# Seven instead of eight half-matrix products in six chunks of a decoder layer's last product

## The chip, the cores and the metric

The kernel runs on one core of one Trainium2 chip. The metric is the device time of one execution in microseconds (us), the median of several runs. Matrix products run on TensorE (PE in the profile, its weight loads PEld), elementwise work on VectorE (DVE) and ScalarE (ACT), and SyncE (SP) issues most transfers from HBM into SBUF. Results of TensorE go to PSUM, which has eight banks of 128 x 512 numbers.

## What is computed

One decoder layer for 256 tokens of width 1024, everything in float32: a norm, one input projection, two kinds of sparse attention, a gated merge with an output projection, and a feed-forward block with a squared ReLU:

```python
x = x + mixed @ w_out[layer]
h2 = rmsnorm(x, norm2_g[layer])
u = jax.nn.relu(h2 @ w_ff1[layer])       # 1024 -> 4096
x = x + (u * u) @ w_ff2[layer]           # 4096 -> 1024
return rmsnorm(x, norm_f_g)
```

The change concerns the product with w_ff2, called the second product here; the one with w_ff1 is the first.

## The kernel before

**Splitting.** TensorE multiplies in a fast format (float32r) that keeps fewer digits. So each operand is split into a high part (ScalarE copies it into the fast format, line 106) and a low part (VectorE takes the difference, line 108), and a product of two matrices is three matmuls, high x high, high x low, low x high (`mm3`, line 219). All of them are issued at line 217.

**Chunks and slots.** The weights come as 60 chunks of 128 x 2048 numbers (1 MB) in the order of the list CHUNKS. Raw chunks, high parts and low parts have three rotating buffers each. A slot is the stretch in which TensorE works on one chunk (`run_slot`, line 202): a list of matmuls, and a list of events, each a function with a position between 0 and 1. An event is issued among the matmuls at its position. That fixes only the order within each engine's queue; an engine starts its next instruction as soon as what it waits for is there. In slot c `split_events` (line 249) puts the splitting of chunk c + 2, in two halves, and then the load of chunk c + 5 into the raw buffer that this frees. In slots 0 to 14 of the second product `std_events` (line 258) calls it with the usual positions.

**The second product.** Its 16 chunks each hold 256 rows of w_ff2, as two row tiles k of 128 x 1024. The left operand, (relu)^2 transposed, lies in the tiles sqh and sql (high, low), written during the first product by `ff1_evac` (line 829), which runs on ScalarE and VectorE in the slot behind its own: ReLU, square in place, high part, low part. A chunk adds, to each of four PSUM banks (two halves t of the tokens times two halves of the columns), the product of two 128 x 128 pieces (k = 0, 1) with 128 x 512 pieces of the weights: eight half-matrix products, 24 matmuls (`ff2_mms`, line 873). In the text B11, B12, B21, B22 are the four 128 x 512 quarters of a chunk and A11 to A22 the four 128 x 128 pieces of the left operand.

**Around it.** In slot 1 `x1_rows` (line 789) transposes the residual x into four PSUM banks (acc0, acc1, tp, yb) and ScalarE copies it to SBUF (line 799). In slot 3 `rstd2` (line 842) squares and sums it on ScalarE; VectorE makes the factors of the norm. Slot 14 covers chunks 14 and 15 together, output part by output part, so that `final_a` (line 886) can add each part to the residual, square it and multiply it with the gain while TensorE is at the next part. `first_part` (line 914) does a quarter of it early. `final_b` (line 902) scales rows and sends them out; GpSimd makes the power in between (line 904). The last part's accumulator is the bank yb.

**Placing.** Some tiles are allocated with unused columns between them ("gap"), so that those behind lie at chosen offsets. The tiles h2h and h2l (left operand of the first product) and sqh and sql come from one pool behind such gaps.

Of the kernel before, what the change touches and what calls it, by code (L numbers as in the profile page):

```python
# [8 lines left out]
F32 = mybir.dt.float32  # L9
F32R = mybir.dt.float32r  # L10
AF = mybir.ActivationFunctionType
ALU = mybir.AluOpType
# [15 lines left out]
    + [("ff2", i, 2048) for i in range(16)]  # L28
)
NCH = len(CHUNKS)  # L30
C_Q, C_QM, C_KM, C_VM, C_GM, C_UPN, C_UPM, C_WOUT, C_FF1, C_FF2 = (
    4, 6, 8, 10, 12, 20, 22, 24, 28, 44)

# [6 lines left out]
def hybrid_layer(ctx: ExitStack, tc: tile.TileContext, gxd, w, w1c, small, const, gf, out):  # L40
    nc = tc.nc
    act, dve, pool, pe = nc.scalar, nc.vector, nc.gpsimd, nc.tensor
# [3 lines left out]
    cp = ctx.enter_context(tc.tile_pool(name="cp", bufs=1))  # L46
# [10 lines left out]
    def bank(tag, name):  # L57
        return ps.tile([128, 512], F32, name=name, tag=tag)
# [8 lines left out]
    def acc_tile():  # L67
        return next_bank("acc")
# [12 lines left out]

    raw, hi, lo = {}, {}, {}

    def raw_tile(c):
        raw[c] = wp.tile([128, 2048], F32, name="raw")

# [5 lines left out]
    def load(c):  # L92
        if c < NCH:
            raw_tile(c)
            load_part(c, 0, 1)

    def split(c, part, parts=2, which=""):
        if c >= NCH:
            return
        n = CHUNKS[c][2]  # L100
        if part == 0 and c not in hi:
            hi[c] = wp.tile([128, 2048], F32R, name="whi")
            lo[c] = wp.tile([128, 2048], F32R, name="wlo")
        a, b = part * n // parts, (part + 1) * n // parts
        if which != "l":
            act.activation(hi[c][:, a:b], raw[c][:, a:b], AF.Copy)  # L106
        if which != "h":
            dve.tensor_tensor(lo[c][:, a:b], raw[c][:, a:b], hi[c][:, a:b].bitcast(F32),  # L108
                              op=ALU.subtract)
# [89 lines left out]
    def at(pos, f, *a):  # L199
        ev.append((pos, f, a))  # L200

    def run_slot(mms):
        n = len(mms)
        es = sorted(ev, key=lambda e: e[0])
        ev.clear()
        j = 0
        for i, m in enumerate(mms):
            while j < len(es) and es[j][0] <= i / n:
                es[j][1](*es[j][2])
                j += 1  # L210
            m()
        while j < len(es):
            es[j][1](*es[j][2])
            j += 1

    def mm(o, l, r, start, stop):
        pe.matmul(o, l, r, start=start, stop=stop, skip_group_check=True)  # L217

    def mm3(o, lh, ll, rh, rl, first, last):
        return [lambda: mm(o, lh, rh, first, False),  # L220
                lambda: mm(o, lh, rl, False, False),
                lambda: mm(o, ll, rh, False, last)]
# [16 lines left out]
    def wstat(o, c, off, nk, ncol, ah, al, ks=None, first=0, last=None):  # L239

        r = []
        last = nk - 1 if last is None else last
        for k in (range(nk) if ks is None else ks):
            a = k * ncol + off
            r += mm3(o, hi[c][:, a:a + 128], lo[c][:, a:a + 128], ah[:, k, :], al[:, k, :],
                     k == first, k == last)
        return r

    def split_events(c, hs, ls):
        for i in range(2):  # L250
            at(hs[i], split, c + 2, i, 2, "h")
        for i in range(2):
            if ls[i] <= 1:
                at(ls[i], split, c + 2, i, 2, "l")
        if ls[1] <= 1:
            at(max(ls) + 0.05, load, c + 5)

    def std_events(c):
        if 9 <= c < 20 and c % 2:
            split_events(c, (0.0, 0.06), (0.09, 0.46))  # L260
        elif 9 <= c < 20:
            split_events(c, (0.0, 0.45), (0.3, 0.8))
        else:
            split_events(c, (0.0, 0.45), (0.3, 0.46))
# [335 lines left out]
    for sec, c0, n in groups:  # L600
# [6 lines left out]
        for i in range(2):  # L607
            c = c0 + i
# [56 lines left out]
    for g in range(4):  # L665
        accs = [acc_tile(), acc_tile()]
        for i in range(2):
            c = C_GM + 2 * g + i
# [40 lines left out]
    for sec, c0, kind, evac in (("upn", C_UPN, "n", upn_evac), ("upm", C_UPM, "m", upm_evac)):  # L709
        for i in range(2):  # L710
            c = c0 + i
# [26 lines left out]
    def two_blocks(c, ah, al, late=8):  # L738

        if late < 8:  # L740
            outs = [acc_tile()[:, 0:256] for _ in range(2)]
            whole = None
            order = [range(late), range(late, 8)]
        else:
            whole = acc_tile()
            outs = [whole[:, 0:256], whole[:, 256:512]]
            order = [range(8)]
        mms = []
        for ks in order:
            for m in range(2):  # L750
                mms += wstat(outs[m], c, m * 128, 8, 256, ah, al, ks=ks, last=7)
        return mms, outs, whole
# [3 lines left out]
    FB = {}  # L756

    def open_ff():
        at_stack.close()
        FB["p"] = ctx.enter_context(tc.tile_pool(name="ff", bufs=1))  # L760
        FB["o"] = ctx.enter_context(tc.tile_pool(name="ps_o", bufs=1, space=PS))
        p = FB["p"]
        p.tile([128, 96], F32, name="gap")
        FB["h2h"] = p.tile([128, 8, 256], F32R, name="h2h")
        FB["h2l"] = p.tile([128, 8, 256], F32R, name="h2l")
        p.tile([128, 16], F32, name="gap2")
        FB["sqh"] = p.tile([128, 32, 256], F32R, name="sqh")
        FB["sql"] = p.tile([128, 32, 256], F32R, name="sql")
        FB["gfb"] = p.tile([128, 1024], F32, name="gfb")
        FB["x1"] = p.tile([128, 2, 1024], F32, name="x1")  # L770
        FB["scr"] = p.tile([128, 1024], F32, name="fscr")
        FB["fst"] = p.tile([128, 24], F32, name="fst")
# [28 lines left out]
    for i in range(4):  # L801
        c = C_WOUT + i
# [20 lines left out]
        else:  # L823
            mms, outs, _ = two_blocks(c, mxh, mxl, 4 if i == 0 else 8)
            run_slot(mms)
            prev = [(wout_evac, (i, outs))]


    def ff1_evac(i, outs, whole):
        r = FB["p"].tile([128, 2, 256], F32, name="ur", bufs=2)  # L830
        rf = r.rearrange("p a q -> p (a q)")
        h, l = (FB[n][:, 2 * i:2 * i + 2, :].rearrange("p a q -> p (a q)") for n in ("sqh", "sql"))
        if whole is None:
            for m in range(2):
                act.activation(r[:, m], outs[m], AF.Relu)
        else:
            act.activation(rf, whole, AF.Relu)  # L837
        dve.tensor_tensor(rf, rf, rf, op=ALU.mult)  # L838
        act.activation(h, rf, AF.Copy)  # L839
        dve.tensor_tensor(l, rf, h.bitcast(F32), op=ALU.subtract)  # L840

    def rstd2():
        fst = FB["fst"]
# [5 lines left out]
    for i in range(16):  # L849
        c = C_FF1 + i  # L850
        if i == 0:
            lo_late(0.03, c - 1)
            split_events(c, (0.1, 0.45), (0.5, 0.5))
        else:
            std_events(c)
        for f, a in prev:
            at(0.02, f, *a)
        mms, outs, whole = two_blocks(c, FB["h2h"], FB["h2l"], 6 if i == 0 else 8)
        run_slot(mms)
        prev = [(ff1_evac, (i, outs, whole))]  # L860
# [3 lines left out]
    PARTS = {0: [(0, 0, 512), (0, 512, 512)], 1: [(1, 0, 512), (1, 512, 512)]}  # L864
    LAST = [(1, 512, 256), (1, 768, 256)]
    ops = {p: FB["o"].tile([128, 512], F32, name=f"o{p[0]}_{p[1]}") for p in PARTS[0] + PARTS[1]}
    whole = ops[PARTS[1][1]]
    ops[LAST[0]] = whole
    fst, x1, scr = FB["fst"], FB["x1"], FB["scr"]
    xo = x1  # L870
    xg = gx[:, 16:].rearrange("p (t d) -> p t d", t=2)

    def ff2_mms(i, p):
        c = C_FF2 + i
        t, c0, n = p
        r = []
        for k in range(2):
            kt = 2 * i + k
            lh, ll = (FB[a][:, kt, t * 128:(t + 1) * 128] for a in ("sqh", "sql"))
            a = k * 1024 + c0  # L880
            r += mm3(ops[p][:, 0:n], lh, ll, hi[c][:, a:a + n], lo[c][:, a:a + n],
                     kt == (28 if p == LAST[1] else 0),
                     kt == (27 if p == PARTS[1][1] else 31))
        return r

    def final_a(p, j):

# [30 lines left out]

    order = PARTS[0] + PARTS[1]
    for i in range(15):  # L920
        std_events(C_FF2 + i)
        for f, a in prev:
            at(0.02, f, *a)
        prev = []
        if i == 1:
            at(0.5, x1_rows, range(4), [acc_tile() for _ in range(3)] + [bank("yb", "yb")])
        if i == 3:
            at(0.1, rstd2)
        if i < 14:
            run_slot([m for p in order for m in ff2_mms(i, p)])  # L930
        else:
            ops[LAST[1]] = bank("yb", "yb")
            at(0.05, first_part)
            at(0.23, final_a, PARTS[0][0], 0)
            at(0.43, final_a, PARTS[0][1], 1)
            at(0.46, final_b, 0)
            at(0.64, final_a, PARTS[1][0], 0)
            at(0.83, final_a, LAST[0], 1)
            run_slot([m for p in PARTS[0] + PARTS[1][:1] + LAST for m in ff2_mms(14, p) + ff2_mms(15, p)])
# [88 lines left out]
```

## Time and profile before

| | us |
|---|---|
| runs: median (lowest to highest of 3) | 380.61 (380.51 to 381.44) |
| the profiled execution | 381.45 |
| its span, first to last instruction | 379.7 |
| TensorE busy in it | 369.5 |
| VectorE busy | 254.5 |
| ScalarE busy | 205.5 |

The profile lists one execution. A row of the timeline has the start (us from the span's start), the duration (us), the engine, the source line, the operation, the tile written and the tiles read, the shape and the number of instructions that the row merges; in brackets stands how long the engine was idle before it and what ended the wait. Ends of matmuls are modelled; starts are measured. The profiled execution is 0.84 us longer than the median run.

The first product takes 197 to 284 us, the second 284 to 373 us.

### The profile page before, as it was taken

To read this page: it belongs to the slowest core of one execution; us is meant where nothing else is said; L and a number is where in the kernel's file an instruction comes from. 1 tells how busy PE (TensorE), PEld (TensorE's weight loads), DVE (VectorE), ACT (ScalarE), POOL (GpSimd) and SP (SyncE) were. 2 spreads that over 40 slices of the span, in tenths; PEclk is the share of its full clock that TensorE was granted. 3 is DMA by queue.
4 is the path that set the end of the run, shared out by engine and by line. 5 is a ranking of instruction groups with operands and counts; after the bars stand their busy time and mean duration, and the time that the engine had idled before them with its cause. 6 is when DMAs were issued, how large, how long until landed. Compare 5 with 4: busy or idle time off the path is not lost.

```text
span 379.7 us, 5935 instructions
## 1 busy us (share of the span) xinstructions
PE 369.5 (97%) x2406; PEld 323.6 (85%) x2406; DVE 254.5 (67%) x397; ACT 205.5 (54%) x360; POOL 5.4 (1%) x15
## 2 busy tenths in 40 slices
PE   6999999999999999999999999999999999999993
PEld 5997878878888788779999999999998888888883
DVE  2978878896966869667868657766676254334435
ACT  5975465767746657343555555565556454433412
POOL 2020000000000000000000000000000000000000
PEclk9999999999999999999999999999999999999998
DMA  7996435333533335440755645554456545654003
GB/s 243 365 370 245 155 127 206 110 112 121 203 121 113 110 125 208 166 167 0 272 230 221 224 163 178 216 218 165 181 215 211 194 161 209 221 173 160 1 2 111
DMA packets 10972, 66.38 MB, mean 175 GB/s; under 512 B 1216, under 2 KB 2752, under 8 KB 3648
## 3 DMA queue, kind: packets, MB, share of 16 engines
q1 hardware_dynamic: 10512, 65.21, 47.2%
q10 hardware_dynamic: 432, 0.79, 0.6%
q8 instruction: 19, 0.31, 0.3%
q14 instruction: 9, 0.07, 0.1%
HBM read 64.94 MB, written 1.05 MB: 174 GB/s over the span
## 4 chain that ended last, share of the span: by engine, by line
PE 88%; DVE 4%; ACT 2%; issue 2%; DMA 1%; POOL 1%; SPq 1%; POOLq 0%; DVEq 0%; ACTq 0%
PE acc L217 53%; PE o L217 22%; PE qacc L217 3%; PE yb L217 2%; PE kvbacc L217 2%; DMA raw<-in_kva_dram 1%; DVE wlo L108 1%; ACT whi L106 1%; PE Sb L508 1%; PE Sa L508 1%; PE Sa L217 1%; PE tp L217 1%; PE Sb L217 1%; PE tp L298 1%; POOL rstd L193 0%
## 5 line engine op out<-in xcount | busy, mean ns | idle before, releaser
L106 ACT ACTIVATE whi<-raw 128x1024 fp32r<-128x1024 f32 (+2 forms) x128 | 123.4, 990 | 98.0 <-PE o L217 35.4
L108 DVE TENSOR_TENSOR wlo<-raw,whi 128x1024 fp32r<-128x1024 f32 (+2 forms) x128 | 141.6, 1138 | 43.3 <-ACT whi L106 43.3
L217 PE MATMUL acc<-h2h,whi 128*128 128x256 f32 x256 | 70.7, 276 | 0.0
L217 PE MATMUL acc<-h2l,whi 128*128 128x256 f32 x256 | 70.7, 276 | 0.0
L217 PE MATMUL acc<-h2h,wlo 128*128 128x256 f32 x256 | 70.7, 276 | 0.0
L217 PE MATMUL acc<-whi,hTh 128*128 128x512 f32 (+1 forms) x128 | 50.9, 398 | 1.7 <-ACT whi L106 1.5
L217 PE MATMUL acc<-wlo,hTh 128*128 128x512 f32 (+1 forms) x128 | 50.5, 395 | 0.4 <-DVE wlo L108 0.2
L217 PE MATMUL acc<-whi,hTl 128*128 128x512 f32 (+1 forms) x128 | 49.5, 387 | 0.0
L217 PE MATMUL o<-whi,sqh 128*128 128x512 f32 (+1 forms) x128 | 49.5, 386 | 0.0
L217 PE MATMUL o<-whi,sql 128*128 128x512 f32 (+1 forms) x128 | 49.4, 386 | 0.0
L217 PE MATMUL o<-wlo,sqh 128*128 128x512 f32 (+1 forms) x128 | 49.4, 386 | 0.0
L217 PEld LDWEIGHTS acc<-h2h,wlo 128*128 128x128 f32 x256 | 48.1, 188 | 0.0
L217 PEld LDWEIGHTS acc<-h2l,whi 128*128 128x128 f32 x256 | 48.1, 188 | 0.0
L217 PEld LDWEIGHTS acc<-h2h,whi 128*128 128x128 f32 x256 | 48.1, 188 | 0.0
L217 PEld LDWEIGHTS acc<-whi,hTh 128*128 128x128 f32 x128 | 24.1, 188 | 8.5 <-ACT whi L106 2.2
L217 PEld LDWEIGHTS acc<-wlo,hTh 128*128 128x128 f32 x128 | 24.1, 188 | 5.0 <-DVE wlo L108 1.1
L217 PEld LDWEIGHTS o<-wlo,sqh 128*128 128x128 f32 x128 | 24.0, 188 | 4.9
L217 PEld LDWEIGHTS o<-whi,sqh 128*128 128x128 f32 x128 | 24.0, 188 | 4.8
L217 PEld LDWEIGHTS o<-whi,sql 128*128 128x128 f32 x128 | 24.0, 188 | 4.8
L217 PEld LDWEIGHTS acc<-whi,hTl 128*128 128x128 f32 x128 | 24.1, 188 | 4.3
L838 DVE TENSOR_TENSOR ur<-ur 128x512 f32<-128x512 f32 x16 | 11.1, 693 | 17.2 <-ACT ur L837 16.2
L840 DVE TENSOR_TENSOR sql<-ur,sqh 128x512 fp32r<-128x512 f32 x16 | 11.1, 693 | 11.2 <-ACT sqh L839 11.2
(249 smaller groups left out, 513.3 us busy)
## 6 DMA issues: line engine op xcount, KB each, us to landing
raw<-in_ff_dram SPq DMA_DIRECT2D x32, 1024.0 KB, 4.8
raw<-in_gm_dram SPq DMA_DIRECT2D x8, 1024.0 KB, 4.8
raw<-in_wout_dram SPq DMA_DIRECT2D x4, 1024.0 KB, 4.7
raw<-in_q_dram SPq DMA_DIRECT2D x2, 1024.0 KB, 6.9
raw<-in_qm_dram SPq DMA_DIRECT2D x2, 1024.0 KB, 8.3
raw<-in_km_dram SPq DMA_DIRECT2D x2, 1024.0 KB, 5.5
raw<-in_vm_dram SPq DMA_DIRECT2D x2, 1024.0 KB, 4.7
raw<-in_upn_dram SPq DMA_DIRECT2D x2, 1024.0 KB, 4.8
```

The lines of the kernel that those rows point to most:

```text
L106: act.activation(hi[c][:, a:b], raw[c][:, a:b], AF.Copy)
L108: dve.tensor_tensor(lo[c][:, a:b], raw[c][:, a:b], hi[c][:, a:b].bitcast(F32), op=ALU.subtract)
L217: pe.matmul(o, l, r, start=start, stop=stop, skip_group_check=True)
L298: pe.transpose(tp[:, j * 256 + t * 128:j * 256 + t * 128 + 128], src[:, t, (2 * i + j) * 128:(2 * i + j + 1) * 128], ident)
L508: pe.transpose(S[x][:, j, c:c + 128], P[:, 2 * x + j, c:c + 128], ident)
L838: dve.tensor_tensor(rf, rf, rf, op=ALU.mult)
L840: dve.tensor_tensor(l, rf, h.bitcast(F32), op=ALU.subtract)
```

## The change

In chunks 2, 4, 6, 8, 10 and 12 of the second product, the 2 x 2 block product is formed with seven products in the form of Winograd and Strassen. The left sums (S1 = A21 + A22, S2 = S1 - A11, S3 = A11 - A21, S4 = A12 - S2) are made in the first product, in the event behind `ff1_evac`, and split into high and low parts; S1 takes the place of A21 in sqh and sql, the others go to the space that the first layers' left operands had. The right sums (T1 = B12 - B11, T3 = B22 - B12, T2 = B22 - T1, and T2 less B21 with its sign turned) are made by VectorE in place in the raw chunk, after B11, B21 and B22 have been split; then they are split into two tiles, th and tl, that take the place of h2h and h2l. Three of the seven products are added to the output banks C11, C12, C21 as before; four (P1, P5, P6, P7) are accumulated over all six chunks in the banks yb, acc0, tp and acc1. In slot 13 `seven_sum` combines these four and adds them to the residual, scaled by the norm's factor. The raw buffer of a seven chunk is loaded anew after its T sums have been split, in the slot before its own. Tiles in the pool are placed anew.

```diff
+SEVEN = (2, 4, 6, 8, 10, 12)
...
+        if seven(c):
+            a, b = ((0, 512), (1024, 2048))[part]
...
-        if ls[1] <= 1:
+        if ls[1] <= 1 and not seven(c + 2):
             at(max(ls) + 0.05, load, c + 5)
...
-        p.tile([128, 96], F32, name="gap")
-        FB["h2h"] = p.tile([128, 8, 256], F32R, name="h2h")
-        FB["h2l"] = p.tile([128, 8, 256], F32R, name="h2l")
-        p.tile([128, 16], F32, name="gap2")
+        p.tile([128, 48], F32, name="gap")
+        for n in "hl":
+            FB["h2" + n] = (p.tile([128, 2176 if n == "h" else 2096], F32R, name="h2" + n, tag="h2" + n)[:, 48:2096]
+                            .rearrange("p (k q) -> p k q", k=8))
+        p.tile([128, 80], F32, name="gap2")
...
+    def s_sums(i, r):
...
+        S = [FB["scr"][:, 128 * a:128 * a + 128] for a in range(4)]
+        A = [[r[:, k, 128 * t:128 * t + 128] for k in range(2)] for t in range(2)]
+        for o, x, y, op in ((0, A[1][0], A[1][1], ALU.add), (2, A[0][0], A[1][0], ALU.subtract),
+                            (1, S[0], A[0][0], ALU.subtract), (3, A[0][1], S[1], ALU.subtract)):
+            dve.tensor_tensor(S[o], x, y, op=op)
+
+    def s_split(i):
+        for h, l, v in ((s_tiles(i, "h")[0], s_tiles(i, "l")[0], FB["scr"][:, 0:128]),
+                        (SS[i, "h"], SS[i, "l"], FB["scr"][:, 128:512])):
+            act.activation(h, v, AF.Copy)
+            dve.tensor_tensor(l, v, h.bitcast(F32), op=ALU.subtract)
+
+    def t_sums(c):
+
+        b = raw[c].rearrange("p (a n) -> p a n", a=4)
+        for o, x, y in ((0, 1, 0), (1, 3, 1), (3, 3, 0), (2, 2, 3)):
+            dve.tensor_tensor(b[:, o], b[:, x], b[:, y], op=ALU.subtract)
+
+    def t_hi(c, a):
+        if a == 0:
+            for n in "hl":
+                TT[n] = FB["p"].tile([128, 2176 if n == "h" else 2096], F32R, name="t" + n, tag="h2" + n)[:, 0:2048]
+        v = slice(1024 * a, 1024 * a + 1024)
+        act.activation(TT["h"][:, v], raw[c][:, v], AF.Copy)
+
+    def t_lo(c, a):
+        v = slice(1024 * a, 1024 * a + 1024)
+        dve.tensor_tensor(TT["l"][:, v], raw[c][:, v], TT["h"][:, v].bitcast(F32),
+                          op=ALU.subtract)
...
+        if i in SEVEN:
+            s_sums(i, r)
...
+        if i - 1 in SEVEN:
+            at(0.55, s_split, i - 1)
...
+    def seven_mms(i):
...
+        for name, a, b in (("P5", S[0], T[0]), ("P7", S[2], T[1]), ("P6", S[1], T[3]),
+                           ("C21", sq(1, 1), T[2]), ("P1", sq(0, 0), B[0]),
+                           ("C11", sq(0, 1), B[2]), ("C12", S[3], B[3])):
+            own = name[0] == "P"
+            r += mm3(PP[name], *a, *b, own and i == SEVEN[0], own and i == SEVEN[-1])
+        return r
+
+    def seven_sum():
+
+        s1 = scr[:, 0:512]
+        u2, u3 = (FB["p"].tile([128, 2, 256], F32, name="ur", bufs=2)
+                  .rearrange("p a q -> p (a q)") for _ in range(2))
+        r0, r1 = fst[:, 4:5], fst[:, 5:6]
+        add = lambda o, v, r: dve.scalar_tensor_tensor(o, v, r, o, op0=ALU.mult, op1=ALU.add)
+        act.activation(s1, PP["P1"], AF.Copy)
+        dve.tensor_tensor(u2, PP["P6"], s1, op=ALU.add)
+        dve.tensor_tensor(u3, PP["P7"], u2, op=ALU.add)
+        add(x1[:, 0, 0:512], s1, r0)
+        add(x1[:, 0, 512:1024], u2, r0)
+        add(x1[:, 0, 512:1024], PP["P5"], r0)
+        add(x1[:, 1].rearrange("p (a n) -> p a n", a=2),
+            u3[:, None, :].to_broadcast([128, 2, 512]), r1)
+        add(x1[:, 1, 512:1024], PP["P5"], r1)
...
-        std_events(C_FF2 + i)
+        c = C_FF2 + i
+        if i == 13:
+            split_events(c, (0.0, 0.1), (0.1, 0.2))
+            at(0.45, seven_sum)
+        else:
+            std_events(c)
...
+        if i + 2 in SEVEN:
+            at(0.62, t_sums, c + 2)
+            at(0.65, t_hi, c + 2, 0)
+            at(0.66, t_hi, c + 2, 1)
+        if i + 1 in SEVEN:
+            for a in range(2):
+                at(0.03, t_lo, c + 1, a)
+            at(0.04, load, c + 4)
...
-        if i < 14:
+        if i in SEVEN:
+            run_slot(seven_mms(i))
+        elif i < 14:
             run_slot([m for p in order for m in ff2_mms(i, p)])
```

## Rows read from the trace of the kernel before

**Rows 1.** The page: busy time by engine, and the chain by engine.
```profile
PE 369.5 (97%) x2406; PEld 323.6 (85%) x2406; DVE 254.5 (67%) x397; ACT 205.5 (54%) x360; POOL 5.4 (1%) x15
...
PE 88%; DVE 4%; ACT 2%; issue 2%; DMA 1%; POOL 1%; SPq 1%; POOLq 0%; DVEq 0%; ACTq 0%
```

**Rows 2.** Two windows: us, then busy PE, PEld, DVE, ACT, POOL, clock, DMA.
```profile
240.00:280.00 40.00, 40.00 (x356) 40.00 (x355) 26.98 (x30) 22.92 (x30) 0.00 (x0) 1.00 0.51 186
300.00:340.00 40.00, 40.00 (x178) 33.13 (x177) 17.43 (x17) 16.27 (x18) 0.00 (x0) 1.00 0.52 187
```

**Rows 3.** Waits, 200 to 373 us: us in total, times, longest.
```profile
ACT whi L106 <- PE o L217: 35.4, 11, 3.4
```

**Rows 4.** Timeline of ScalarE in the second product.
```profile
313.48 2.01 ACT L106 ACTIVATE whi<-raw 128x1024 fp32r<-128x1024 f32 x2 [3.43 <-PE o L217]
318.92 2.01 ACT L106 ACTIVATE whi<-raw 128x1024 fp32r<-128x1024 f32 x2 [3.43 <-PE o L217]
```

**Rows 5.** Timeline of TensorE in the second product.
```profile
300.36 0.39 PE L217 MATMUL o<-whi,sqh 128*128 128x512 f32 x1
...
300.58 0.39 PE L217 MATMUL o<-wlo,sqh 128*128 128x512 f32 x1
```

**Rows 6.** Timeline of VectorE from slot 13 to the end.
```profile
358.09 2.36 DVE L108 TENSOR_TENSOR wlo<-raw,whi 128x1024 fp32r<-128x1024 f32 x2 [3.08 <-ACT whi L106]
362.44 0.48 DVE L916 SCALAR_TENSOR_TENSOR x<-o,fst,x 128x256 f32<-128x256 f32 x1 [1.99 <-PE o L217]
365.16 0.75 DVE L891 SCALAR_TENSOR_TENSOR x<-o,fst,x 128x512 f32<-128x512 f32 x1 [2.24 <-PE o L217]
...
366.70 0.15 DVE L898 TENSOR_SCALAR fst<-fst 128x1 f32<-128x1 f32 x1
367.88 0.75 DVE L891 SCALAR_TENSOR_TENSOR x<-o,fst,x 128x512 f32<-128x512 f32 x1 [1.02 <-PE o L217]
...
370.31 0.75 DVE L911 TENSOR_SCALAR gx<-gx,fst 128x384 f32<-128x384 f32 x2 [0.73 <-POOL fst L904]
...
373.09 0.43 DVE L896 TENSOR_TENSOR gx<-x,gfb 128x256 f32<-128x256 f32 x1
373.47 0.48 DVE L891 SCALAR_TENSOR_TENSOR x<-yb,fst,x 128x256 f32<-128x256 f32 x1
```

**Rows 7.** Timeline of TensorE, its last two products.
```profile
373.03 0.28 PE L217 MATMUL yb<-wlo,sqh 128*128 128x256 f32 x1
373.15 0.28 PE L217 MATMUL yb<-whi,sql 128*128 128x256 f32 x1
```

**Rows 8.** Timeline of VectorE at the end of the first product.
```profile
280.55 0.69 DVE L838 TENSOR_TENSOR ur<-ur 128x512 f32<-128x512 f32 x1 [1.08 <-ACT ur L837]
...
282.56 2.36 DVE L108 TENSOR_TENSOR wlo<-raw,whi 128x1024 fp32r<-128x1024 f32 x2
```

**Rows 9.** Timeline of ScalarE at the end of the first product.
```profile
281.28 0.63 ACT L839 ACTIVATE sqh<-ur 128x512 fp32r<-128x512 f32 x1 [0.76 <-DVE ur L838]
```

**Rows 10.** Timeline of ScalarE in slots 1 to 3 of the second product.
```profile
293.10 1.58 ACT L799 ACTIVATE x<-acc 128x512 f32<-128x512 f32 x3 [1.10 <-PE acc L797]
...
297.21 2.01 ACT L106 ACTIVATE whi<-raw 128x1024 fp32r<-128x1024 f32 x2 [2.04 <-issue]
...
303.56 1.04 ACT L845 ACTIVATE fscr<-x 128x1024 f32<-128x1024 f32 x1
...
305.79 1.04 ACT L106 ACTIVATE whi<-raw 128x1024 fp32r<-128x1024 f32 x1
```

**Rows 11.** The page, DMA issues: count, KB each, median us to landing.
```profile
raw<-in_ff_dram SPq DMA_DIRECT2D x32, 1024.0 KB, 4.8
```

**Rows 12.** Timeline of TensorE at 52 us, in an earlier projection.
```profile
52.72 0.40 PE L217 MATMUL acc<-wlo,hTh 128*128 128x512 f32 x1
52.95 0.40 PE L217 MATMUL acc<-whi,hTl 128*128 128x512 f32 x1
53.19 0.39 PE L217 MATMUL acc<-whi,hTh 128*128 128x512 f32 x1
```

More of the change, by code (lines that the diff above doesn't have):

```diff
@@ L82, in hybrid_layer, with seven @@
     raw, hi, lo = {}, {}, {}
+    def seven(c):
+        return c >= C_FF2 and c - C_FF2 in SEVEN
     def raw_tile(c):
@@ L826, in hybrid_layer, with s_tiles @@
             prev = [(wout_evac, (i, outs))]
+    SS, TT = {}, {}
+    def s_tiles(i, n):
+        return [FB["sq" + n][:, 2 * i, 128:256]] + [
+            SS[i, n][:, 128 * a:128 * a + 128] for a in range(3)]
+    def s_sums(i, r):
+        if not SS:
+            FB["p"].tile([128, 40], F32, name="gap3")
+            for n, e in (("h", 128), ("l", 16)):
+                SS[n] = cp.tile([128, 2048 + e], F32R, name="s" + n, tag="act" + n.upper())
+                SS[n + "x"] = FB["p"].tile([128, 384], F32R, name="sx" + n)
+        j = SEVEN.index(i)
+        for n in "hl":
+            SS[i, n] = (SS[n][:, 16 + 384 * j:400 + 384 * j] if j < 5 else SS[n + "x"])
+        S = [FB["scr"][:, 128 * a:128 * a + 128] for a in range(4)]
[14 more added lines that the diff above has]
+        if a == 0:
+            for n in "hl":
+                TT[n] = FB["p"].tile([128, 2176 if n == "h" else 2096], F32R, name="t" + n, tag="h2" + n)[:, 0:2048]
[5 more added lines that the diff above has]
+                          op=ALU.subtract)
     def ff1_evac(i, outs, whole):
@@ L869, in hybrid_layer @@
     fst, x1, scr = FB["fst"], FB["x1"], FB["scr"]
+    PP = {"C11": ops[PARTS[0][0]], "C12": ops[PARTS[0][1]], "C21": ops[PARTS[1][0]]}
     xo = x1
@@ L884, in ff2_mms @@
         return r
+    def seven_mms(i):
+        c = C_FF2 + i
+        sq = lambda t, k: tuple(FB[a][:, 2 * i + k, t * 128:(t + 1) * 128] for a in ("sqh", "sql"))
+        S = list(zip(*(s_tiles(i, n) for n in "hl")))
+        B = [tuple(w[c][:, 512 * a:512 * a + 512] for w in (hi, lo)) for a in range(4)]
+        T = [tuple(TT[n][:, 512 * a:512 * a + 512] for n in "hl") for a in range(4)]
+        r = []
+        for name, a, b in (("P5", S[0], T[0]), ("P7", S[2], T[1]), ("P6", S[1], T[3]),
[19 more added lines that the diff above has]
+        add(x1[:, 1, 512:1024], PP["P5"], r1)
     def final_a(p, j):
@@ L920, in hybrid_layer @@
     for i in range(15):
-        std_events(C_FF2 + i)
+        c = C_FF2 + i
+        if i == 13:
[3 more added lines that the diff above has]
+            std_events(c)
         for f, a in prev:
@@ L924, in hybrid_layer @@
         prev = []
+        if i + 2 in SEVEN:
[6 more added lines that the diff above has]
+            at(0.04, load, c + 4)
+        if i == SEVEN[0]:
+            PP.update((n, bank(t, n)) for n, t in
+                      (("P5", "acc0"), ("P7", "acc1"), ("P6", "tp"), ("P1", "yb")))
         if i == 1:
```

## The prediction

> **What bounds the kernel now.** I read the page first. TensorE is busy for 97% of the span and holds 88% of the chain that ended last [rows 1]; nothing else comes near. A busy TensorE is not yet one at its pace, so I went on to the stretches: in the first feed-forward product (240 to 280 us) and in the second (300 to 340 us) TensorE is busy all the time at a granted clock of 1.00, VectorE for 27.0 and 17.4 of 40 us, ScalarE for 22.9 and 16.3 [rows 2]. A look at who waits in 200 to 373 us has no line in which TensorE is the one that waits; its most frequent line is ScalarE waiting for TensorE [rows 3]. In the second product ScalarE's two copies start every 5.44 us, each time released by the end of an older chunk's products [rows 4]: that is the length of a slot. Two matmuls that follow each other inside start 0.22 us apart [rows 5], and 5.44/24 = 0.2267 us is their mean pace. So in this stage a product removed is 0.2267 us removed, as long as operands come in time. The tail is different. Behind the last product VectorE's chain sets the end: from 370.31 us on its instructions follow each other closely, and the last output part starts at 373.47, while its last product, started at 373.15 for 0.28, ends at 373.43 [rows 6, 7]. VectorE and TensorE arrive together there; whoever is later moves the end.
>
> **Removed.** A chunk of the second product has 8 half-matrix products (512 columns) of three matmuls; six chunks (2, 4, ... 12) get 7. That is 6 x 3 = 18 matmuls x 0.2267 = **4.08 us** off TensorE. A seven slot lasts 21 x 0.2267 = 4.76 us. The Trainium skill, "TensorE: Matmul & The Clock Gate", section "Back-to-back issue gap", gives about 131 ns for a matmul of 512 columns in a stream of weight loads and matmuls, by which the saving would be 2.4 us. The trace does not agree for these matmuls: 227 ns.
>
> **Added in the first product's slots (S sums).** In six slots VectorE gets four sums of 128 columns and two low parts of 128 and 384. VectorE took 0.69 for 512 columns and 0.43 for 256 [rows 6, 8], so I estimate 0.30 for 128 (between the 0.15 of a single column and the 0.43) and 0.56 for 384: 4 x 0.30 + 0.86 = 2.1 us. ScalarE adds about 0.9. VectorE's usual work there is 27.0/40 x 5.44 = 3.7 us a slot, so such a slot needs 5.8 of 5.44, the next one 3.7. Over two slots that is 9.5 of 10.9, and a chunk's halves are made two slots ahead. Cost 0; the cover is that lead of over 5 us. Without it the excess of 0.4 us a slot would show, 2 us in all.
>
> **Added in the second product (T sums and their halves).** For a pair of slots (seven, then ordinary; 4.76 + 5.44 = 10.20 us) VectorE has: the low half of the three B quarters still needed 0.69 + 1.18, four in-place sums of 512 columns 4 x 0.69, two T low halves 2.36, the next ordinary chunk's 2.36 [rows 8]. Sum 9.35 of 10.20: busy, not over. The order in time, from the start of slot s-2: the split starts 0.9 (the buffer comes free 0.2 after the slot's start, since a matmul lasts 0.39 [rows 5] at a pace of 0.2267; ScalarE's 512 columns take 0.63 [rows 9]) and ends about 3.05; sums to 5.8; T high parts on ScalarE to 6.9; T low to 7.0 and 8.2; the ordinary chunk's low to 10.55. Slot s starts at 10.20 and its first two groups need only the first T half, ready at 7.0; the third needs the second half at 11.6, ready at 8.2. **Slack is over 3 us**, and the next pair's split is wanted at 11.1, VectorE free at 10.55, so nothing piles up. New waits on TensorE's side: the single T buffer is written again after the seven slot's fourth group (2.7 us into the slot), before the sums are done, so it holds up nobody.
> Two places are tighter. (a) Slot 2: its four new accumulators are the banks of the x1 transposes. ScalarE copies three of them in 1.58 us from 293.10 on [rows 10], the fourth makes it 2.1. Now two T parts and the two copies of chunk 3 stand ahead of them. Low halves start at 282.56 in the last slot of the first product [rows 8], so at 288.0 one slot later; 1.87 of split and 2.76 of sums end at 292.6, the T parts at 293.7, chunk 3's copies at 295.7, the x1 copies at 297.7. Slot 2 starts at 297.0 (ScalarE's next release is 297.21 [rows 10], 0.2 into it) and wants the second-copied bank (free about 296.7), 0.7 later the third (297.2), 2.7 later the fourth. It fits by 0.3; beyond that, a few tenths once. (b) Slot 3: the squares take ScalarE 2.2 us [rows 10] ahead of chunk 5's second half, and VectorE's reciprocal, behind them, holds its queue. VectorE falls some 2 us behind; the T halves of chunk 6 still come over 1 us early. Cost of both 0.
>
> **The loads.** A seven chunk's raw buffer is freed only after its T low halves, so load s+3 is issued one slot later than now, just ahead of load s+4. SP has only loads queued behind it. A load takes 4.8 us to land [rows 11]. Issued 8.2 after the start of slot s-2, chunk s+3 lands at 13.0; its split starts with slot s+1 at 15.0. If both loads share the engines it may be 2 us later and touches the split, not TensorE, which needs the halves a slot later. Cost 0; without the cover one load's wait, some 2 us per pair.
>
> **The combination in slot 13.** One ScalarE copy and seven VectorE instructions: two sums of 512 (0.69), four multiply-adds of 512 (0.75 as in the output step), one of 1024 (1.18 + 0.07): 5.6 us. They queue behind chunk 15's low halves, which end at 358.09 + 2.36 = 360.45 in the old time [rows 6], so they end at 366.1, and the early output part (0.48) at 366.55. The first output step stood at 365.16: it is 1.4 us late. From its start to the end of its last small instruction passed 1.69 us (365.16 to 366.85), so VectorE is free at 368.25 and the next step starts at 368.28 instead of 367.88: **0.40 us late**. From there the chain to 373.47 has no spare, so the end moves by it. Bounds: at the closest spacing that rows show (0.04 less per instruction) 0.1; with each instruction dearer by a tenth 1.0. A gain below 0 is excluded, since the last product still ends where it does.
>
> **Sum.** -4.08 + 0.40 = -3.7 us. The profiled execution took 381.45 us (span 379.7), 0.84 above the median of 380.61, so the sum made there gives 377.8; carried to the median it is **376.9**. Its own range is 376.2 to 377.8: the tail's bounds, and a few tenths in slot 2 or between runs.
>
> **Rivals.** *VectorE becomes the bound* (second product). For it: 92% of the pair. Against: the added sums would have to cost 17% more (0.85 of 5.1 us) before a pair overruns, the square in place, the same form, took 0.69 [rows 8], and the slack of 3 us comes on top. At 35% dearer each pair overruns by 0.9; five pairs less the slack is 1.5 us, and the tail some 0.4: 378.8.
> *The new operands stream slower.* The pace is not the same everywhere: at 52.72 to 53.19 starts lie 0.23 to 0.24 apart with the same forms, and the last products of 256 columns start 0.12 apart, 0.24 for 512 [rows 7, 12]. The T and S tiles lie elsewhere, and nothing of before shows their pace. If only the 126 products of seven slots took 0.240, 126 x 0.0133 = 1.7 comes back: 378.6. Against: all operands of the slots from 297 on keep 0.2267, whichever buffer they use.
> *The other side: the moved tiles slow the whole second product.* The change shifts sqh and sql by 192 words, so all its products get other stationary places. At 0.240 some 354 of 512 columns cost 4.7 more: 381.6, slower than before. It decides from 3.7/354 = 10.5 ns, a pace of 0.237, which the rows at 52 us just reach [rows 12]. Against: that stretch stands between transposes, and the slots without them show no such pace.
> *Nothing gained:* what the products leave free is filled by a wait that I don't see (a buffer released late, six times 0.6 us): 380.6.
>
> **Chances.** Forecast 0.75, VectorE as bound 0.08, slower new operands 0.08, whole product slower 0.05, nothing gained 0.04. The range 376.1 to 378.9 holds the first three but their far ends. A measurement can tell about 0.3%, 1.1 us, from no change: faster (below 379.5) 0.75 + 0.08 + 0.06 = 0.89; same 0.05; slower 0.06.
>
> **What would show it.** Right: 18 matmuls fewer, ScalarE's releases in the second product 4.76 and 5.44 us apart in turn, no line with TensorE waiting, VectorE near 90% busy between slots 2 and 12, and the second output step a few tenths later against slot 14's start. Wrong: TensorE waiting for VectorE's tl or ScalarE's th at the start of a seven slot (VectorE as bound), starts 0.23 to 0.24 apart (operands), an early output part later than 4.4 us after slot 14's start (tail).

## The result and the profile after

The changed kernel takes **377.14 us** (median of 4 runs, 376.78 to 377.62) against 380.72 before (4 runs, 380.51 to 381.44). The ratio is 0.9903, with a 95% interval from 0.9886 to 0.9921: faster by 3.6 us, about 1%. Its profiled execution took 377.16 us at a span of 375.4. In the new kernel all matmuls are issued at line 224, the high copies at 113, the low parts at 115.

The page shows 18 matmuls fewer on TensorE, and 40 us more of work on VectorE:

```profile
PE 366.3 (98%) x2388; PEld 320.8 (85%) x2388; DVE 295.1 (79%) x476; ACT 220.5 (59%) x385; POOL 5.4 (1%) x15
```

The windows answer to [rows 2] (columns as there): the first product, and the slots from 2 to 13.

```profile
240.00:280.00 40.00, 40.00 (x355) 40.00 (x355) 32.52 (x50) 26.07 (x37) 0.00 (x0) 1.00 0.51 185
296.59:357.79 61.20, 61.20 (x272) 50.69 (x271) 52.51 (x59) 34.76 (x40) 0.00 (x0) 1.00 0.49 184
```

TensorE never pauses in the 61.2 us, at full clock, while VectorE is busy for 52.5 of them. The waits of 190 to 375 us have no line in which TensorE or its weight loads wait.

To see where the time went I cut the span at two products: the first of the second product (chunk 0) and the first of slot 14. The timeline of TensorE before:

```profile
284.28 0.39 PE L217 MATMUL o<-whi,sqh 128*128 128x512 f32 x1
...
362.24 0.39 PE L217 MATMUL o<-whi,sqh 128*128 128x512 f32 x1
```

and after:

```profile
283.91 0.39 PE L224 MATMUL o<-whi,sqh 128*128 128x512 f32 x1
...
357.79 0.39 PE L224 MATMUL o<-whi,sqh 128*128 128x512 f32 x1
```

This **stretch** is 77.95 us before and 73.88 after: 4.08 shorter (from unrounded starts), which is 18 x 0.2267. From slot 14's start to the span's end it is 17.42 before (379.66 - 362.24) and 17.58 after (375.37 - 357.79): the tail is 0.16 longer. The remaining 0.37 us of the difference of the spans lies ahead of the second product and is run against run: the first product itself takes 87.04 us in both.

VectorE in the tail (timeline; answers to [rows 6]): the seven instructions of the combination, the early output part, the output steps.

```profile
353.69 2.36 DVE L115 TENSOR_TENSOR wlo<-raw,whi 128x1024 fp32r<-128x1024 f32 x2 [2.40 <-ACT whi L113]
355.97 0.68 DVE L975 TENSOR_TENSOR ur<-P,fscr 128x512 f32<-128x512 f32 x1
...
360.71 0.75 DVE L973 SCALAR_TENSOR_TENSOR x<-P,fst,x 128x512 f32<-128x512 f32 x1
361.57 0.48 DVE L1014 SCALAR_TENSOR_TENSOR x<-o,fst,x 128x256 f32<-128x256 f32 x1
361.97 0.74 DVE L989 SCALAR_TENSOR_TENSOR x<-o,fst,x 128x512 f32<-128x512 f32 x1
...
363.63 0.74 DVE L989 SCALAR_TENSOR_TENSOR x<-o,fst,x 128x512 f32<-128x512 f32 x1
```

The first output step starts 4.18 us after slot 14's start (2.92 before), the second 5.85 (5.64 before).

### The profile page after: what moved, and what is told of

It reads as the page before. It is cut to its first block, busy times and chain, and to the rows that moved or that the text cites. A ratio compares the mean times of both kernels' runs of the same rounds, so it can differ in the third digit from the quotient of the medians.

```text
span 375.4 us, 6004 instructions
## 1 busy us (share of the span) xinstructions
PE 366.3 (98%) x2388; PEld 320.8 (85%) x2388; DVE 295.1 (79%) x476; ACT 220.5 (59%) x385; POOL 5.4 (1%) x15
## 4 chain that ended last, share of the span: by engine, by line
PE 82%; DVE 7%; ACT 4%; DMA 2%; issue 2%; SPq 1%; POOL 1%; POOLq 0%; DVEq 0%; ACTq 0%
PE acc L224 52%; PE o L224 13%; PE P L224 4%; PE qacc L224 3%; DMA raw<-in_kva_dram 2%; PE yb L224 2%; DVE wlo L115 2%; ACT whi L113 2%; DVE x L973 1%; PE Sa L515 1%; PE Sb L515 1%; PE Sa L224 1%; PE Sb L224 1%; PE tp L305 1%; PE tp L224 1%
## 5 line engine op out<-in xcount | busy, mean ns | idle before, releaser
L113 ACT ACTIVATE whi<-raw 128x1024 fp32r<-128x1024 f32 (+3 forms) x128 | 120.6, 969 | 55.0 <-PE acc L224 33.7
L115 DVE TENSOR_TENSOR wlo<-raw,whi 128x1024 fp32r<-128x1024 f32 (+3 forms) x128 | 138.4, 1113 | 15.4 <-ACT whi L113 15.3
L224 PE MATMUL o<-whi,sqh 128*128 128x512 f32 (+1 forms) x86 | 33.1, 385 | 0.0
L224 PE MATMUL o<-whi,sql 128*128 128x512 f32 (+1 forms) x86 | 33.0, 384 | 0.0
L224 PE MATMUL o<-wlo,sqh 128*128 128x512 f32 (+1 forms) x86 | 33.0, 384 | 0.0
L883 ACT ACTIVATE th<-raw 128x1024 fp32r<-128x1024 f32 x12 | 12.8, 1062 | 19.2 <-DVE raw L876 19.2
L224 PEld LDWEIGHTS o<-whi,sql 128*128 128x128 f32 x86 | 16.2, 188 | 3.2
L224 PEld LDWEIGHTS o<-whi,sqh 128*128 128x128 f32 x86 | 16.2, 188 | 3.2
L224 PEld LDWEIGHTS o<-wlo,sqh 128*128 128x128 f32 x86 | 16.2, 188 | 3.1
```

What stands on the lines that cost most here:

```text
L883: act.activation(TT["h"][:, v], raw[c][:, v], AF.Copy)
```

## The experiments

Each is an edit of the changed kernel. Times are medians, ratios are against the kernel before measured on the same chip in the same job; the stretch and the tail are from the one profiled execution of each. The medians of two jobs differ for the kernel before too (380.72 us with the result, 381.59 and 381.27 in the two jobs below), and a ratio is not the quotient of the two medians (with the T tiles moved by 16 words it is 0.9881, the quotient 0.9921). So effects under about 1 us are read from the traces.

**Three chunks instead of six.**

```diff
-SEVEN = (2, 4, 6, 8, 10, 12)
+SEVEN = (2, 4, 6)
```

> Only chunks 2, 4 and 6 take seven products. Theory (the gain is the removed matmuls at their pace, 0.2267 us each, less a fixed tail of about 0.16): 9 matmuls fewer than before, so the stretch from the first product of the last stage to slot 14 is 77.95 - 2.04 = 75.91 us, against 73.88 with six chunks; the time about 378.8 to 379.2, half way. Rival (the gain comes from elsewhere, the placing or a fixed effect of the new order): the same as with six chunks, about 377.1.

Measured: 379.37 us, ratio 0.9929 (0.9897 to 0.9960). Stretch 359.64 - 283.72 = 75.92 us, tail 17.54. Half the removed matmuls give half the gain in the stretch, and the tail's price stays. The median lies 0.17 us above the range that I gave from the earlier runs; the interval of the ratio holds half the change's gain (0.9952) and the whole (0.9903) alike, so it is the stretch that tells them apart. The rival falls.

**The eighth product put back.** It leaves every sum in place and issues the product for C11 a second time, so that the output is another.

```diff
                            ("C11", sq(0, 1), B[2]),
+                           ("C11", sq(0, 1), B[2]),
                            ("C12", S[3], B[3])):
```

> The six seven chunks issue the product for C11 twice, so they have 24 matmuls again with all the sums still made (C11's second addend counts double). Theory: TensorE's matmuls alone set the stage, so 18 x 0.2267 = 4.08 us come back: stretch 77.95, time 381.0 to 381.3, a trifle above the kernel before. Rival (VectorE or the loads pace the slots): the extra matmuls go partly into waits and the time rises by less than 3 us.

Measured: 381.37 us, ratio 0.9979 (0.9951 to 1.0008). Stretch 362.12 - 284.17 = 77.95 us, the value before, tail 17.58. So with slots of the old length the sums, the splits and the later loads cost TensorE nothing, and what the change takes off is the matmuls. That they cost nothing in the shorter slots too is seen in the change itself, which gains the whole 4.08 and has no wait. Against the kernel before (381.59 in this job), the runs don't show a difference; the median is just above the range expected.

**More work on VectorE.** One or three sums of 512 columns per seven chunk, thrown away. The edit shown is that of three; with one it has range(1).

```diff
         b = raw[c].rearrange("p (a n) -> p a n", a=4)
+        u = FB["p"].tile([128, 2, 256], F32, name="ur", bufs=2).rearrange("p a q -> p (a q)")
+        for _ in range(3):
+            dve.tensor_tensor(u, b[:, 2], b[:, 0], op=ALU.subtract)
```

With one:

> VectorE makes one sum of 512 columns more per seven chunk (thrown away), 0.66 us. Theory (a free 1.05 us per pair and a lead): a pair needs 9.8 of 10.20; the T halves of chunk 6, which came 1.9 us early with the change, come about 0.6 early, and the x1 copies ahead of slot 2 still fit by 0.2. Nothing waits: stretch from the first product of the last stage to slot 14 73.9 us, time as with the change, 377 to 378. Rival (the change already stands at VectorE's limit): waits at slots 2 and 6 and over 1 us longer.

Measured: 378.28 us, ratio 0.9915 (0.9884 to 0.9945). Stretch 357.84 - 283.88 = 73.96 us, 0.08 over the change's. One wait appears, a weight load of slot 2:

```profile
PEld P L224 <- ACT x L807: 0.2, 1, 0.2
```

It is the place that the prediction called tight, the x1 copies (line 807 now). The first T half of chunk 6 ended at 316.98, slot 6 started at 317.04: in time, but by 0.06 us and not by 0.6. With the change it ended at 315.05, so it came 1.93 later, which is about the three added sums of chunks 2, 4 and 6 in full (0.65 each), where I had reckoned 1.3. The theory holds, with both margins smaller than I said. The median is 1.1 us above the change's, more than the trace accounts for. By the ratios the difference is 0.0012, about 0.5 us, and the intervals overlap.

With three:

> VectorE makes three sums of 512 columns more per seven chunk (thrown away), 1.95 us. Theory (VectorE's queue took 9.15 us of the 10.20 of a pair when it was never idle, so 1.05 is free, and the T halves come 1.9 to 3.7 us early): a pair now needs 11.1, 0.9 over; the lead is used up by slot 6 and from there VectorE is the bound: 3 to 5 us longer than with the change, 380 to 382, with TensorE waiting for tl at the starts of slots 6 to 12. Rival (VectorE has plenty left, at 79% busy over the span): no change, 377.1.

Measured: 386.22 us, ratio 1.0088 (1.0046 to 1.0129): slower than the kernel before. Stretch 365.53 - 283.91 = 81.62 us, 7.75 over the change's. The theory's kind is right, its size is not. The waits of 296 to 366 us (total, times, longest) show more than VectorE's low halves:

```profile
PE P L224 <- DVE tl L890: 2.1, 3, 0.9
...
PE P L224 <- ACT th L886: 1.3, 1, 1.3
PE P L224 <- ACT x L807: 1.2, 1, 1.2
```

and the timeline of TensorE at the start of slot 6 shows what came behind the waits:

```profile
318.30 0.39 PE L224 MATMUL o<-whi,sql 128*128 128x512 f32 x1
319.98 0.49 PE L224 MATMUL P<-th,sqh 128*128 128x512 f32 x1 [1.29 <-ACT th L886]
321.42 0.50 PE L224 MATMUL P<-tl,sqh 128*128 128x512 f32 x1 [0.94 <-DVE tl L890]
...
323.02 0.63 PE L224 MATMUL P<-th,sh 128*128 128x512 f32 x1
323.44 0.63 PE L224 MATMUL P<-tl,sh 128*128 128x512 f32 x1
```

From 322.6 to 325.5 us matmuls start 0.43 us apart, twice the usual. The windows name the cause, the granted clock:

```profile
318.40:322.40 4.00, 1.76 (x7) 1.02 (x6) 3.93 (x5) 3.19 (x4) 0.00 (x0) 0.99 0.01 2
322.60:325.50 2.90, 2.90 (x8) 2.30 (x7) 2.90 (x4) 2.08 (x3) 0.00 (x0) 0.50 0.59 181
326.50:340.00 13.50, 13.50 (x61) 11.16 (x61) 13.19 (x18) 5.49 (x6) 0.00 (x0) 1.00 0.57 225
```

TensorE was busy for 1.76 of 4.0 us, then ran at 0.50 (1.2 GHz) for about three, then at 1.00 (2.4 GHz) again. The Trainium skill, "TensorE: Matmul & The Clock Gate", section "HAM oscillation — how this bites in real kernels", tells of a kernel that waits for a DMA ahead of each group of products, and whose products behind the wait run throttled. Here the waits are shorter ones for ScalarE and VectorE; the trace agrees that half the clock follows (0.50). Taken from the starts, TensorE loses the 7.75 us like this: 1.5 at slot 2 (1.63 and 0.34 in place of two paces), 2.8 at slot 6 (1.68, 1.44 and 0.34 in place of three), 1.6 of half clock and its edges, 0.6 at slot 10, 1.1 at slot 12 and small ones of starts up to 0.24 apart.

What sets the sum of these is VectorE's queue and not the clock. Its timeline:

```profile
310.88 0.17 DVE L913 TENSOR_SCALAR fst<-fst 128x2 f32<-128x2 f32 x1 [1.94 <-ACT fscr L912]
...
315.18 2.14 DVE L877 TENSOR_TENSOR ur<-raw 128x512 f32<-128x512 f32 x3
...
320.14 2.43 DVE L890 TENSOR_TENSOR tl<-raw,th 128x1024 fp32r<-128x1024 f32 x2
...
326.50 2.14 DVE L877 TENSOR_TENSOR ur<-raw 128x512 f32<-128x512 f32 x3
...
354.11 2.43 DVE L890 TENSOR_TENSOR tl<-raw,th 128x1024 fp32r<-128x1024 f32 x2
```

Chunk 6's first T half ends at 321.36, 6.31 us later than with the change. That is nearly all of the 6.5 that the added sums of chunks 2, 4 and 6 take, because VectorE's waits for ScalarE stay (1.94 ahead of the factors of the norm in both runs). Slot 6 had a lead of 1.93, so it is 4.37 late. From 311.17 us until behind the halves of chunk 12 VectorE is never idle, and a pair takes it 11.32 us (326.50 - 315.18) instead of the 10.20 of TensorE: three pairs to slot 12 add 3.37. Together that is 7.74 us, all that was lost, and the half clock falls inside it. The times of the ten runs agree: in four the mean granted clock of the whole run was 0.996 or 0.997, as in the change's runs (0.995 to 0.998), and in six 0.989 to 0.991 (0.991 in the profiled one). The four took 385.59 to 390.74 us and the six 385.39 to 386.48. So no run shows that the half clock costs time here. The tail is 18.61 us, 1.03 longer than with the change: ScalarE waits 2.29 us for the load of chunk 15, which is issued behind the T halves of chunk 12, and the low halves ahead of the combination come that much later.

So VectorE's limit is close: 2 us per pair beyond the change lose all of the gain and more.

**The T tiles 16 words further, and 32.**

```diff
-                TT[n] = FB["p"].tile([128, 2176 if n == "h" else 2096], F32R, name="t" + n, tag="h2" + n)[:, 0:2048]
+                TT[n] = FB["p"].tile([128, 2176 if n == "h" else 2096], F32R, name="t" + n, tag="h2" + n)[:, 16:2064]
```

> The T tiles lie 16 words further on in the same space; the work is the same. Theory A (the place of the streamed operand doesn't set the pace): all products stay at 0.2267, 377.1. Theory B (it does): the 72 matmuls that stream T take up to 0.240, which is 72 x 0.0133 = 1.0 us more, 378.1; the starts in the trace tell even if the time can't.

Measured with 16: 378.56 us, ratio 0.9881 (0.9828 to 0.9935). Stretch 358.40 - 283.97 = 74.43 us, 0.56 over the change's, with no wait. Slot 10's first matmuls, after the change:

```profile
337.39 0.39 PE L224 MATMUL P<-th,sqh 128*128 128x512 f32 x1
337.61 0.39 PE L224 MATMUL P<-tl,sqh 128*128 128x512 f32 x1
337.84 0.39 PE L224 MATMUL P<-th,sql 128*128 128x512 f32 x1
```

and with the shift:

```profile
337.81 0.40 PE L224 MATMUL P<-th,sqh 128*128 128x512 f32 x1
338.05 0.40 PE L224 MATMUL P<-tl,sqh 128*128 128x512 f32 x1
338.29 0.39 PE L224 MATMUL P<-th,sql 128*128 128x512 f32 x1
```

0.24 between starts in place of 0.22 or 0.23. Unrounded, the starts lie 0.225 to 0.237 apart in the seven slots, also for products that don't stream T, while most of the ordinary slots keep 0.2267. The product for C12, for one, has neither operand moved, and its starts lie up to 0.236 apart: a product's own two places don't settle its pace alone. Theory B in kind, at half its size. The other shift is [:, 32:2080] in the same line:

> The T tiles lie 32 words further on instead of 16. Theory A (what matters is the place within a stretch of 32 words): all products back at 0.2267, stretch 73.9. Theory B (any place but the first costs): stretch 74.4 as with 16 words.

Measured: 378.22 us, ratio 0.9928 (0.9900 to 0.9956); stretch 358.60 - 284.21 = 74.40 us. Theory A falls: 32 words cost the same 0.5 us as 16, with starts of 0.224 to 0.238 in the seven slots.

**The left operand and all behind it 16 words further.**

```diff
-        p.tile([128, 80], F32, name="gap2")
+        p.tile([128, 96], F32, name="gap2")
```

> All tiles from sqh on lie 16 words further; the work is the same. Theory A (moving the T tiles by 16 words made the products that stream T, and those next to them, start up to 0.237 us apart, so the place of the stationary operand against the streamed one matters too): the products with sqh and sql get slower, stretch 0.5 to 4 us over 73.9. Theory B (only the streamed operand's place matters): stretch 73.9, all starts 0.2267 apart.

Measured: 379.32 us, ratio 0.9942 (0.9917 to 0.9968). Stretch 361.47 - 285.70 = 75.77 us, 1.89 over the change's: nearly half of the gain, with no wait and a granted clock of 1.00. Now the products of seven slots and of ordinary ones start 0.225 to 0.236 apart. A pair of slots takes 10.47 us, as ScalarE's releases show (timeline; first halves of chunks 10 and 12):

```profile
330.28 1.58 ACT L113 ACTIVATE whi<-raw 128x512 fp32r<-128x512 f32 x2 [1.85 <-issue]
...
340.75 1.58 ACT L113 ACTIVATE whi<-raw 128x512 fp32r<-128x512 f32 x2 [1.85 <-issue]
```

After the change the same two are 10.20 apart:

```profile
327.43 1.58 ACT L113 ACTIVATE whi<-raw 128x512 fp32r<-128x512 f32 x2 [1.38 <-issue]
...
337.63 1.58 ACT L113 ACTIVATE whi<-raw 128x512 fp32r<-128x512 f32 x2 [1.59 <-issue]
```

Theory A holds: the place of the stationary operand changes the pace too. Some tiles that are no operand of these products moved along (x1, the scratch tile, the buffers of `ff1_evac`), and no run moves them alone. The shift doesn't only cost: the last products of 256 columns start 0.113 us apart here and 0.120 with the change.

**The early output part behind the second step.**

```diff
-            at(0.05, first_part)
             at(0.23, final_a, PARTS[0][0], 0)
             at(0.43, final_a, PARTS[0][1], 1)
+            at(0.45, first_part)
```

> The early output part is issued behind the second output step, into the time in which VectorE waits for GpSimd's power, instead of ahead of the first step; same work. Theory (the sums in slot 13 queue the output steps, and from the second step on the lateness reaches the end): the first step starts 0.4 us earlier against slot 14, the second at 5.64 instead of 5.85, the end 17.42 us after slot 14's start instead of 17.58. The time gains 0.16 us, which the runs can't tell. Rival (the end is set elsewhere): 17.58 stays.

Measured: 377.33 us, ratio 0.9892 (0.9871 to 0.9913). Slot 14 starts at 358.75. VectorE's timeline:

```profile
362.34 0.74 DVE L989 SCALAR_TENSOR_TENSOR x<-o,fst,x 128x512 f32<-128x512 f32 x1
...
364.39 0.75 DVE L989 SCALAR_TENSOR_TENSOR x<-o,fst,x 128x512 f32<-128x512 f32 x1 [0.30 <-PE o L224]
...
366.01 0.48 DVE L1014 SCALAR_TENSOR_TENSOR x<-o,fst,x 128x256 f32<-128x256 f32 x1
```

The second step now waits for TensorE, 5.64 after slot 14's start as before the change, and the early part (line 1014) sits in the wait for GpSimd. The first step starts 3.59 after slot 14's start, 0.59 earlier than with the change, where I expected 0.4. The tail is 17.43 us (376.17 - 358.75), 0.15 shorter than with the change: the theory, to a hundredth. This version is the change without its price in the tail; the runs can't tell the two apart.

## Why the prediction was right

Forecast 376.9 (376.1 to 378.9), measured 377.14. The mechanism came as forecast; that the numbers lie 0.24 apart is in part luck. By the two traces the change is worth 4.08 - 0.16 = 3.92 us, by the medians 3.58, and the runs of the change alone spread over 0.84 us.

- **Removed: 4.08 us.** The stretch shrank by 4.08; a pair of slots takes 10.20 us (TensorE's slots 6, 7 and 8 start at 316.99, 321.75 and 327.19, 4.76 and 5.44 apart); three chunks give half, the eighth product takes all of it back. This step is shown. ScalarE's releases, which I had named as the sign, show only the 10.20, since its copies of the ordinary chunks stand behind the T parts.
- **S sums in the first product, cost 0.** The first product takes 87.04 us in both traces. The sums of 128 columns took 0.28 to 0.29 (I estimated 0.30).
- **T sums, cost 0.** In the one pair in which VectorE's queue never ran empty it needed 9.15 us, not 9.35: merged rows follow each other a little closer than durations add up. Slack was about what I said: the first T half came 3.0 to 3.7 us early in five of the six chunks, and 1.9 in chunk 6, behind the squares (315.05 against slot 6's start at 316.99). Between slots 2 and 12 VectorE was busy for 45.8 of 51.0 us, the 90% that I had named. But the range of the rival was too mild: I priced VectorE as the bound at 1.5 us for 35% dearer sums. The run with three more sums, 38% on top of the 5.1 us, lost 7.75. I had priced only what a pair overruns, less a lead of 3 us; in the run the sums of the first three chunks came on top almost in full, since VectorE's waits for ScalarE there didn't shrink, and the lead at slot 6 was 1.9.
- **Loads, cost 0.** TensorE waits for nothing there. In the run with the eighth product they are issued by the same rule, and its stretch is that of before. A late load does show in the run with three more sums, where chunk 15 holds up ScalarE for 2.29 us.
- **The combination: 0.40 late, measured 0.21 at the second step and 0.16 at the end.** The mechanism is shown by the last experiment, the size was over. The first step came 4.18 us after slot 14's start, against the 4.30 of my sum (366.54 - 362.24): seven instructions took 5.5 us where I added 5.6, and the early part ran straight on. From the first step to the second passed 1.66 instead of 1.72. I also held that from the second step on lateness passes whole to the end; 0.05 of it was lost on the way.
- **The rival of the moved tiles.** It was a real one: a shift of 16 words costs 0.6 or 1.9 us here. I gave it small chances since the slots of before all kept one pace, but that said nothing of the new places. The rows at 52 us, which I read as just reaching a pace of 0.237, give 0.235. That the change's own places keep 0.2267 could not be seen in the trace of before, and the forecast leant on it.

What stays open is by which rule places set the pace; three shifts don't give it.

## What to carry to other kernels

Where a stretch of the trace shows TensorE without a single wait at a fixed pace, removed matmuls are worth their number times the pace (here 18 x 0.2267 us), and replacing them by sums on another engine pays only while that engine has room in each pair of slots, not on average over the span (VectorE at 80% of the span lost more than the gain). Count that room against the queue's busy time, and don't count idle time that is itself a wait for another engine: sums added ahead of such waits came on top almost in full. A fallen clock behind a wait need not be the cause of a loss: see first whether the engine waited for was ever idle. When tiles move, compare starts of matmuls to a few nanoseconds before and after; a changed pace shows there and in no wait.

## What the runs showed of the hardware

- The pace of matmuls of 512 columns depends on where stationary and streamed tiles lie: 0.2267 us with the change's places, up to 0.238 with the T tiles moved by 16 or 32 words, 0.225 to 0.236 with the stationary tiles moved by 16. The Trainium skill, "TensorE: Matmul & The Clock Gate", section "Step-by-step: what each phase is for", says that the two operands are read through independent ports and that loading weights takes nothing from the running matmul. It says nothing of where the tiles lie. If the two reads never met, one would expect the shift of sqh to cost nothing; 1.89 us were measured.
- Two waits at slot 6 that left TensorE busy for 1.76 of 4.0 us were followed by three microseconds at a granted clock of 0.50. VectorE set the time there, and no run shows that the clock cost any.
